# A Strassen-form input projection with attention pipelined over heads, in a two-layer hybrid decoder

## The chip, the cores and the metric

The kernel runs on one core of a Trainium2 chip. The time is the device time of one launch in microseconds (us), median of several runs; lower is better. Five engines work side by side, each in the order of its own queue: TensorE (PE, with its weight loads listed as PEld), VectorE (DVE), ScalarE (ACT), GpSimd (POOL) and SyncE (SP, which issues the DMAs).

## The reference, cut to what matters

```python
D_MODEL, SEQ, DEPTH = 2048, 512, 2            # 8 heads; q rank 512, kv rank 256, rope 64
h = layernorm(x, emb_ln_g, emb_ln_b)
for l in range(DEPTH):
    proj = h @ w_in[l]                        # 512 x 2048 @ 2048 x 4928
    (q_lat, kv_lat, k_rope, g_mla, p_in, g_pool, c_h, c_b, c_c, g_conv) = split(proj)
    y_mla  = mla_mixer(q_lat, kv_lat, k_rope, ...) * silu(g_mla)      # causal attention, 8 heads
    y_pool = pool_mixer(p_in, w_pool, pool_scale) * silu(g_pool)      # windows 2, 4, 8, 16
    y_conv = conv_mixer(c_h, c_b, c_c, conv_w) * silu(g_conv)         # b * conv3(c * h)
    out = concat(y_mla, y_pool, y_conv) @ w_out[l] + b_out[l]
    h = layernorm(ALPHA * h + out, ln_g[l], ln_b[l])
```

All numbers are float32. Of the 4928 columns of `w_in`, 4608 are 18 pairs of 128-column tiles (q 2 pairs, attention gate 4, pooling 4, convolution 8), and 320 are the kv latent and the rotary key.

## The kernel before, in words

Every large product is made from two float32r parts of each operand: `split` (L79) has ACT cast to the high part and DVE subtract it for the low part, and `mm3` (L99) issues three matmuls (lines L101, L102, L103): high times high, high times low, low times high. The 128 x 128 stationary operand is loaded anew for each.

The normalised residual lies transposed, features on partitions, in `XH` and `XL`: 16 row tiles of 128 features by 512 tokens. Weights come in blocks of 1024 columns per partition through `unit` (L83): SP loads a `raw` tile (2 buffers), ACT casts, DVE subtracts, into a ring `dunit` of 5. `in_steps` (L167) makes a pair of column tiles: four such units, 16 row tiles, two `bankA` accumulators, 96 matmuls of 512 columns:

```python
for k in range(KT):                     # 16 row tiles
    if kk == 0: wh, wl = in_unit(l, col, u)
    for e in range(2):                  # two column tiles, 512 tokens each
        mm3(accs[e], wh[:, kk, es], wl[:, kk, es], XH[:, k, :], XL[:, k, :], k == 0, k == KT - 1)
    yield
```

Layer by layer: `kv_proj` (L198) makes the kv latent with tokens on partitions; two q pairs follow. Then the heads run in a written-out order (L560 to L591): `scores` (L499, softmax per block of 128 queries: L509 to L517), `turn` (L520, the transposes L524 and the split of the probabilities), `do_k`, `do_q`, `do_rope`, `do_v` and `attend` (L537). Between these, `F(n)` (L350) lets the generators in `fill` issue steps of projections that nothing waits for: the four pairs of attention gates and the first pooling pair. After the heads come the other eleven pairs with the pooling and convolution arithmetic between them (`pooled_of` L612, L663 to L686), then the output projection, 4 token tiles by 2048 columns, with residual on POOL (`resid` L706), then layer norm. The last 256 columns go one token tile at a time, so that the next layer's transposes (`ln_to_x` L133) run beside them at the places `TURN_AT` and beside `kv_proj`.

In the embedding's layer norm the first token tile is normalised, transposed and projected while the others are still loaded (L277 to L297). Nothing but `xn_dram`, the normalised residual, goes out to DRAM between.

## Time and profile before

| what | value |
|---|---|
| runs | 1485.55, 1485.9, 1486.29 us; median 1485.9 |
| profiled execution | span 1470.5 us from first to last instruction; the launch's time of the runs is 15.4 us above this span |
| PE | 1437.9 us busy, 98%, 7202 matmuls |
| DVE | 708.3 us, 48%, 1185 instructions |
| ACT | 553.0 us, 38%, 863 |
| POOL | 215.4 us, 15%, 193 |
| DMA | 160.51 MB, 109 GB/s |

The profiled execution has no time of its own beside its span; the 15.4 us around it are taken from the median. Busy time of an engine counts overlapping instructions once. A matmul's own duration is longer than the distance to the next one, so the cost of a run of matmuls is read from their start times.

### The profile page before, as it was taken

What the parts mean: (1) busy time and instruction counts of PE and PEld (TensorE: products, weight loads), DVE (VectorE), ACT (ScalarE), POOL (GpSimd) and SP (SyncE); (2) the same over time, 40 slices, a digit from 0 to 9 for tenths busy, and PEclk for the clock granted to TensorE, in tenths of its full rate; (3) what the DMA queues carried; (4) which work ended last, traced back from release to release, by engine and by line L of the source; (5) the groups of instructions that cost most, each with busy time, mean ns of one, the idle gap of its engine ahead of it and who ended that gap; (6) DMA issues with size and microseconds to landing.
All of it is one profiled execution on the core that took longest, in us unless ns stands there. A gap on an engine that the chain in (4) does not pass through costs nothing.

```text
span 1470.5 us, 18166 instructions
## 1 busy us (share of the span) xinstructions
PE 1437.9 (98%) x7202; PEld 1225.9 (83%) x7202; DVE 708.3 (48%) x1185; ACT 553.0 (38%) x863; POOL 215.4 (15%) x193
## 2 busy tenths in 40 slices
PE   6999999999999999999999999999999999999995
PEld 6888888888888888888998888888888888888895
DVE  7745666553232253534563465666432323524338
ACT  7636466442222233212253375545232222512211
POOL 3011000012000005800001100000300000094004
PEclk9999999999999999999999999999999999999998
DMA  8522223133333345533433232132433333733333
GB/s 290 147 84 76 69 80 85 47 107 100 87 100 100 97 128 193 164 105 114 145 103 99 73 92 58 51 86 66 114 100 99 90 99 101 251 118 118 101 115 115
DMA packets 131104, 160.51 MB, mean 109 GB/s; under 512 B 13920, under 2 KB 109388, under 8 KB 127948
## 3 DMA queue, kind: packets, MB, share of 16 engines
q1 hardware_dynamic: 131020, 159.36, 35.6%
q8 instruction: 56, 0.92, 0.3%
q14 instruction: 28, 0.23, 0.1%
HBM read 146.76 MB, written 12.58 MB: 108 GB/s over the span
## 4 chain that ended last, share of the span: by engine, by line
PE 77%; issue 10%; POOL 5%; DVE 4%; ACT 3%; DMA 1%; SPq 0%; ACTq 0%; DVEq 0%; POOLq 0%
PE bankA L101 20%; PE bankA L102 20%; PE bankA L103 20%; PE bankB L103 5%; PE bankB L101 5%; PE bankB L102 5%; POOL M L711 2%; POOL M L710 2%; PE bankB L524 1%; PE bankB L142 1%; POOL scr L345 1%; DVE M L787 1%; ACT scr L514 1%; POOL scr L344 1%; DVE dunit L81 1%
## 5 line engine op out<-in xcount | busy, mean ns | idle before, releaser
L81 DVE TENSOR_TENSOR dunit<-raw,dunit 128x1024 fp32r<-128x1024 f32 (+2 forms) x229 | 291.0, 1273 | 475.6 <-ACT dunit L80 475.6
L101 PE MATMUL bankA<-XH,dunit 128*128 128x512 f32 x1152 | 451.3, 392 | 0.0
L103 PE MATMUL bankA<-XH,dunit 128*128 128x512 f32 x1152 | 449.1, 390 | 0.0
L102 PE MATMUL bankA<-XL,dunit 128*128 128x512 f32 x1152 | 449.0, 390 | 0.0
L80 ACT CAST dunit<-raw 128x1024 fp32r<-128x1024 f32 (+2 forms) x229 | 237.3, 1038 | 548.7 <-PE bankA L103 383.6
L103 PEld LDWEIGHTS bankA<-XH,dunit 128*128 128x128 f32 x1152 | 216.2, 188 | 45.2
L102 PEld LDWEIGHTS bankA<-XL,dunit 128*128 128x128 f32 x1152 | 216.4, 188 | 42.7
L101 PEld LDWEIGHTS bankA<-XH,dunit 128*128 128x128 f32 x1152 | 216.3, 188 | 42.4
L101 PE MATMUL bankA<-dunit,XH 128*128 128x512 f32 (+1 forms) x376 | 139.0, 370 | 1.0 <-ACT XH L80 1.0
L102 PE MATMUL bankA<-dunit,XH 128*128 128x512 f32 (+1 forms) x376 | 138.0, 367 | 1.0 <-POOL dunit L244 1.0
L103 PE MATMUL bankA<-dunit,XL 128*128 128x512 f32 (+1 forms) x376 | 138.0, 367 | 0.0
L710 POOL TENSOR_TENSOR M<-M,ag 128x512 f32<-128x512 f32 x32 | 48.3, 1538 | 270.6 <-ACT ag L700 270.6
L103 PE MATMUL bankB<-dunit,XL 128*128 128x512 f32 (+1 forms) x256 | 86.0, 336 | 0.0
L102 PE MATMUL bankB<-dunit,XH 128*128 128x512 f32 (+1 forms) x256 | 86.0, 336 | 0.0
L101 PE MATMUL bankB<-dunit,XH 128*128 128x512 f32 (+1 forms) x256 | 86.0, 336 | 0.0
L101 PEld LDWEIGHTS bankA<-dunit,XH 128*128 128x128 f32 x376 | 71.3, 190 | 11.7 <-ACT XH L80 1.7
L102 PEld LDWEIGHTS bankA<-dunit,XH 128*128 128x128 f32 x376 | 71.4, 190 | 11.2 <-POOL dunit L244 1.3
L103 PEld LDWEIGHTS bankA<-dunit,XL 128*128 128x128 f32 x376 | 71.2, 189 | 10.4 <-DVE XL L81 0.4
L344 POOL TENSOR_TENSOR scr<-scr,sinT 128x512 f32<-128x512 f32 x10 | 13.0, 1297 | 275.2 <-ACT scr L341 257.1
L101 PEld LDWEIGHTS bankB<-dunit,XH 128*128 128x128 f32 x256 | 48.6, 190 | 5.1
L102 PEld LDWEIGHTS bankB<-dunit,XH 128*128 128x128 f32 x256 | 48.6, 190 | 5.0
L103 PEld LDWEIGHTS bankB<-dunit,XL 128*128 128x128 f32 x256 | 48.6, 190 | 5.0
(200 smaller groups left out, 1834.7 us busy)
## 6 DMA issues: line engine op xcount, KB each, us to landing
raw<-in_w_in_dram SPq DMA_DIRECT2D x144, 512.0 KB, 3.8
raw<-in_w_out_dram SPq DMA_DIRECT2D x64, 512.0 KB, 3.8
M<-xn_dram SPq DMA_DIRECT2D x8, 1024.0 KB, 4.9
xn_dram<-M SPq DMA_DIRECT2D x6, 1024.0 KB, 4.3
raw<-in_w_ukv_dram SPq DMA_DIRECT2D x8, 512.0 KB, 3.8
raw<-in_w_uq_dram SPq DMA_DIRECT2D x32, 128.0 KB, 2.3
...
```

The source lines that it names most:

```text
L80: nc.scalar.copy(hi, src)
L81: nc.vector.tensor_sub(lo, src, hi.bitcast(F32))
L101: nc.tensor.matmul(acc, lhsT=ah, rhs=bh, start=first, stop=False)
L102: nc.tensor.matmul(acc, lhsT=ah, rhs=bl, start=False, stop=False)
L103: nc.tensor.matmul(acc, lhsT=al, rhs=bh, start=False, stop=last)
L142: nc.tensor.transpose(out=ps[:, (n * j + i) * P:(n * j + i + 1) * P], in_=rs[i][:, k // 4, (k % 4) * P:(k % 4 + 1) * P], identity=ident)
L344: nc.gpsimd.tensor_mul(sw, sw, sinT)
L345: nc.gpsimd.tensor_add(res, res, sw)
L514: nc.scalar.activation(pe[:, :W], s[:, :W], AF.Exp, bias=st[:, 1:2], scale=rs[:, qb:qb + 1], accum_out=st[:, 2:3])
L524: nc.tensor.transpose(out=pt[:, j * P:(j + 1) * P], in_=pe[:, j * P:(j + 1) * P], identity=ident)
L710: nc.gpsimd.tensor_mul(rt[t][:, cs], rt[t][:, cs], ag[:, cs])
L711: nc.gpsimd.tensor_add(rt[t][:, cs], rt[t][:, cs], ab[:, cs])
```

## The change

The tokens are halved (256 each), a pair's columns are halved (128 each), the 16 row tiles are halved into even and odd ones. Each pair is then a 2 x 2 by 2 x 2 block product, made with Strassen's seven products instead of eight. The sums of input blocks are made once per layer (`turn_steps`, `sums`: `A11`, `S5` from the first token half; `S2`, `N22`, `S1`, `S7`, `S6` once the second half is there), those of weights in every unit (`unit_of`: three POOL sums through two `sm` buffers, four splits), and `finish` puts the output blocks together from four banks, five DVE instructions and two ACT copies. For the first four pairs the products 5 and 3, which need the first token half alone, are made ahead (`pre_steps`, `prefix`) while the second half is turned; `pair_steps` then makes the other five.

All 18 pairs now come before attention, q last. Pooling and convolution results (`mix_dram`) and attention gates (`gate_dram`) go to DRAM and are loaded again. Attention has no projection between; `prep` of head h+2 and `scores` of head h+1 stand around `attend` of head h. One arena `AR` and seven blocks of 16 KB take the place of the pools. The output projection starts with the pooling and convolution rows.

```diff
-            for e in range(2):
-                es = slice(e * P, (e + 1) * P)
-                mm3(accs[e], wh[:, kk, es], wl[:, kk, es], XH[:, k, :], XL[:, k, :], k == 0, k == KT - 1)
...
+    rawp = ctx.enter_context(tc.tile_pool(name="rawp", bufs=3))
+    smp = ctx.enter_context(tc.tile_pool(name="smp", bufs=2))
+    tqp = ctx.enter_context(tc.tile_pool(name="tqp", bufs=6))
+    tdp = ctx.enter_context(tc.tile_pool(name="tdp", bufs=2))
...
+        E1, O1 = eo(1)
+        comb("S2", ALU.add, E1, O1)
...
+        comb("S1", ALU.add, E0, O1)
+        comb("S7", ALU.subtract, O0, O1, nc.vector)
+        comb("S6", ALU.subtract, E1, E0)
...
+        else:
+            t0 = tq()
+            v = t0.rearrange("p i (k q c) -> p i k q c", k=2, q=2)
+            split(v[:, 0], v[:, 1], rq[:, :, 0::3])
...
+            s = smt()
+            sv = s.rearrange("p (k n) -> p k n", k=2)
+            nc.gpsimd.tensor_sub(sv, raw.rearrange("p (k h n) -> p k h n", k=2, h=2)[:, :, 0],
+                                 raw.rearrange("p (k h n) -> p k h n", k=2, h=2)[:, :, 1])
+            t1 = tq()
+            split(t1[:, 0, :], t1[:, 1, :], s)
...
+        s = smt()
+        nc.gpsimd.tensor_add(s[:, :256].rearrange("p (k c) -> p k c", k=2), rq[:, :, 0], rq[:, :, 3])
+        t2 = tdp.tile([P, 2, 256], F32R, name="td", tag="td")
+        split(t2[:, 0, :], t2[:, 1, :], s[:, :256])
...
+        nc.gpsimd.tensor_add(s.rearrange("p (a c) -> p a c", a=4), rw[:, :, 0], rw[:, :, 1])
+        t3 = tq()
+        split(t3[:, 0, :], t3[:, 1, :], s)
...
+    def product(banks, q, w, j):
+        b, side = BANK[q]
+        bh, bl = [S[XOF[q]][:, i, j, :] for i in range(2)]
+        mm3(banks[b][:, 256 * side:256 * (side + 1)], w[0], w[1], bh, bl,
+            j == 0 and q in OPENS, j == 7 and q in CLOSES)
...
+        for u in range(4):
+            W = unit_of(l, col, u, rest)
+            for k in range(2):
+                for q in "24176" if rest else "5234176":
+                    product(banks, q, W[q][k], 2 * u + k)
+                yield
...
+        nc.scalar.copy(EG[:, 1:3], two[0])
+        nc.scalar.copy(EG[:, 0::3], two[1])
+        nc.vector.tensor_add(cv[:, 1], EG[:, 0], EG[:, 3])
+        nc.vector.tensor_add(cv[:, 2], EG[:, 1], EG[:, 2])
+        nc.vector.tensor_sub(EG[:, 0:2], EG[:, 0:2], EG[:, 2:4])
+        nc.vector.tensor_add(cv[:, 0::3], two[2], EG[:, 0:2])
+        nc.vector.tensor_add(cv[:, 0::3], cv[:, 0::3],
+                             banks[3][:, 0:256].unsqueeze(1).broadcast_to([P, 2, 256]))
...
+        for h in range(NH):
+            for qb in range(4):
+                turn(h, qb)
+            if h + 1 < NH:
+                for qb in range(4):
+                    scores(h + 1, qb)
+            attend(h)
+            if h + 2 < NH:
+                prep(h + 2)
```

How the order of instructions moves, at three places.

DVE, in the convolution pairs of the first layer. `dunit` and `raw` are the weight unit and its load, `uc` and `mscr` the convolution's tiles. Before:

```order
L81 TENSOR_TENSOR dunit<-raw,dunit 128x1024 x8
L671 TENSOR_TENSOR uc<-bankA,mscr 128x512 x2
L674 TENSOR_SCALAR mscr<-uc,vec 128x512 x2
L675 SCALAR_TENSOR_TENSOR mscr<-uc,vec,mscr 128x512 x2
L676 SCALAR_TENSOR_TENSOR mscr<-uc,vec,mscr 128x512 x2
L81 TENSOR_TENSOR dunit<-raw,dunit 128x1024 x4
```

Of the change, for the same pair (L333 to L337 are `finish`, L116 the subtraction in `split`):

```order
L116 TENSOR_TENSOR tq<-raw,tq 128x512
L334 TENSOR_TENSOR AR<-AR 128x256
L333 TENSOR_TENSOR AR<-AR 128x256
L335 TENSOR_TENSOR AR<-AR 128x512
L116 TENSOR_TENSOR tq<-sm,tq 128x512
L336 TENSOR_TENSOR AR<-bankB,AR 128x2x256
L116 TENSOR_TENSOR td<-sm,td 128x256
L337 TENSOR_TENSOR AR<-AR,bankB 128x2x256
L116 TENSOR_TENSOR tq<-sm,tq 128x512
L557 TENSOR_TENSOR AR<-AR 128x512 x2
L560 TENSOR_SCALAR AR<-AR,vec 128x512 x2
L561 SCALAR_TENSOR_TENSOR AR<-AR,vec 128x512 x2
```

One subtraction of 1024 columns per unit became four, of 512, 512, 256 and 512, three of them from a POOL sum (`sm`); `finish` is new, and the convolution reads its gate from SBUF (`AR`) where it read a bank.

POOL, from the last pooling sums to the residual in the first layer. Before:

```order
L622 TENSOR_TENSOR ps_3110<-ps_3107 128x524
L621 MEMSET ps_3113 128x8
L622 TENSOR_TENSOR ps_3113<-ps_3110 128x520
L670 MEMSET uc 128x2 x2
L710 TENSOR_TENSOR M_80<-M_80,ag 128x512
```

Of the change, two units within that stretch (L267, L274, L280 are the three sums of `unit_of`):

```order
L267 TENSOR_TENSOR sm<-raw 128x512
L274 TENSOR_TENSOR sm<-raw 128x256
L556 MEMSET AR 128x2
L494 MEMSET AR 128x1
L494 MEMSET AR 128x2
L556 MEMSET AR 128x2
L494 MEMSET AR 128x8
L280 TENSOR_TENSOR sm<-raw 128x512
```

POOL had nothing but two small fills between the pooling and the residual; now every unit of every pair has three sums there.

PE, between two blocks of scores of one head. `kh`, `qnh` and so on are keys and queries, `XH` with `dunit` is a projection. Before:

```order
L508 MATMUL bankB<-KL,SB 128x256
L101 MATMUL bankA<-XH,dunit 128x512
L102 MATMUL bankA<-XL,dunit 128x512
L103 MATMUL bankA<-XH,dunit 128x512
L101 MATMUL bankA<-XH,dunit 128x512
L102 MATMUL bankA<-XL,dunit 128x512
L103 MATMUL bankA<-XH,dunit 128x512
L101 MATMUL bankB<-kh,qnh 128x384
```

Of the change (`KQ` holds keys and queries, `RR` the rotary queries, L724 are transposes of probabilities):

```order
L706 MATMUL bankA<-KHL,RR 128x256
L707 MATMUL bankA<-KHL,RR 128x256
L120 MATMUL bankA<-KQ 128x256
L121 MATMUL bankA<-KQ 128x256
L724 MATMUL bankB<-ct,AR 128x128 x4
L122 MATMUL bankA<-KQ 128x256
L706 MATMUL bankA<-KHL,RR 128x256
L707 MATMUL bankA<-KHL,RR 128x256
L120 MATMUL bankA<-KQ 128x384
```

The projection steps that stood between two blocks of scores are gone; the only other matmuls there are the same head group's transposes.

## Rows read from the trace of the kernel before

**Rows 1.** The page: span, busy time by engine, clock, chain by engine.

```profile
span 1470.5 us, 18166 instructions
...
PE 1437.9 (98%) x7202; PEld 1225.9 (83%) x7202; DVE 708.3 (48%) x1185; ACT 553.0 (38%) x863; POOL 215.4 (15%) x193
...
PEclk9999999999999999999999999999999999999998
...
PE 77%; issue 10%; POOL 5%; DVE 4%; ACT 3%; DMA 1%; SPq 0%; ACTq 0%; DVEq 0%; POOLq 0%
```

**Rows 2.** Windows: start, the dense middle, tail; columns as the first line says.

```profile
core 0: us, PE busy (x) PEld busy (x) DVE busy (x) ACT busy (x) POOL busy (x), PEclk, DMA share, GB/s
0.00:15.00 15.00, 3.99 (x18) 3.49 (x18) 7.47 (x18) 6.62 (x10) 3.31 (x10) 1.00 0.85 284
15.00:1452.30 1437.30, 1433.93 (x7185) 1222.41 (x7185) 687.12 (x1149) 543.33 (x850) 203.90 (x178) 1.00 0.35 107
1452.30:1470.50 18.20, 0.00 (x0) 0.00 (x0) 13.70 (x19) 3.04 (x4) 8.20 (x6) 0.61 0.33 124
```

**Rows 3.** Timeline of PE, output projection: start us, duration us, instruction.

```profile
645.98 0.39 PE L101 MATMUL bankA<-dunit,XH 128*128 128x512 f32 x1
...
646.66 0.39 PE L101 MATMUL bankA<-dunit,XH 128*128 128x512 f32 x1
...
689.90 0.28 PE L101 MATMUL bankB<-dunit,XH 128*128 128x256 f32 x1
...
690.26 0.28 PE L101 MATMUL bankB<-dunit,XH 128*128 128x256 f32 x1
```

**Rows 4.** Windows: heads with their five pairs; the other eleven pairs.

```profile
100.00:306.00 206.00, 204.84 (x1055) 173.82 (x1054) 121.92 (x280) 115.94 (x212) 16.61 (x13) 1.00 0.25 70
306.00:545.00 239.00, 239.00 (x1060) 198.02 (x1059) 85.64 (x97) 61.83 (x73) 14.48 (x26) 1.00 0.36 100
```

**Rows 5.** DVE groups by line: count, then busy us, mean ns, idle before.

```profile
L81 DVE TENSOR_TENSOR dunit<-raw,dunit 128x1024 fp32r<-128x1024 f32 x216 | 279.6, 1297 | 449.4 <-ACT dunit L80 449.4
L81 DVE TENSOR_TENSOR XL<-M,XH 128x512 fp32r<-128x512 f32 x32 | 21.6, 689 | 8.9 <-ACT XH L80 8.9
...
L675 DVE SCALAR_TENSOR_TENSOR mscr<-uc,vec,mscr 128x512 f32<-128x512 f32 x8 | 5.6, 746 | 0.0
...
L674 DVE TENSOR_SCALAR mscr<-uc,vec 128x512 f32<-128x512 f32 x8 | 3.5, 479 | 0.0
L717 DVE TENSOR_TENSOR M<-bankA,M 128x256 f32<-128x256 f32 x8 | 3.3, 417 | 7.1 <-PE bankA L103 7.1
```

**Rows 6.** POOL: six sums of 512 columns in a row; two more sizes by line.

```profile
587.69 7.54 POOL L711 TENSOR_TENSOR M<-M,ab 128x512 f32<-128x512 f32 x6
...
L345 POOL TENSOR_TENSOR scr<-scr 128x512 f32<-128x512 f32 x10 | 19.8, 1977 | 2.9 <-DVE scr L343 2.1
...
L244 POOL TENSOR_TENSOR dunit<-kvraw,dunit 128x320 fp32r<-128x320 f32 x6 | 5.0, 867 | 3.4 <-ACT dunit L241 3.4
```

**Rows 7.** Timeline of POOL and DVE in the last layer norm, both at SBUF operands.

```profile
1438.63 1.55 POOL L782 TENSOR_TENSOR M<-M,dunit 128x512 f32<-128x512 f32 x1 [1.12 <-ACT M L780]
1440.26 1.62 POOL L783 TENSOR_TENSOR M<-M,dunit 128x512 f32<-128x512 f32 x1
...
1440.65 1.78 DVE L782 TENSOR_TENSOR M<-M,dunit 128x512 f32<-128x512 f32 x1
1442.46 0.69 DVE L783 TENSOR_TENSOR M<-M,dunit 128x512 f32<-128x512 f32 x1
```

**Rows 8.** The same two engines at 607 us, DVE with one operand in PSUM.

```profile
607.83 0.67 DVE L717 TENSOR_TENSOR M<-bankA,M 128x512 f32<-128x512 f32 x1
...
607.89 1.29 POOL L711 TENSOR_TENSOR M<-M,ab 128x512 f32<-128x512 f32 x1
```

**Rows 9.** Timeline of PE: a block's transposes in attention; the start.

```profile
210.86 0.63 PE L524 MATMUL bankB<-ct,scr 128*128 128x128 f32 x4 [0.24 <-DVE scr L517]
...
8.07 0.28 PE L250 MATMUL bankB<-ct,ve 32*128 32x32 f32 x1 [8.07 <-DMA ct<-in_consts_dram]
10.27 3.68 PE L142 MATMUL bankB<-ct,M 128*128 128x128 f32 x16 [1.91 <-ACT M L227]
14.97 0.64 PE L101 MATMUL bankA<-dunit,XH 128*128 128x320 f32 x1 [1.03 <-ACT XH L80]
```

**Rows 10.** DMA issues on the page: KB each, us to landing.

```profile
raw<-in_w_in_dram SPq DMA_DIRECT2D x144, 512.0 KB, 3.8
```

More of the change, by code (lines that the diff above doesn't have):

```diff
@@ L125, in ln_stats, with tok @@
         return mv[:, 0:1], rstd
[L127 to L145 removed]
+    def tok(t, c=None):
+        return ar(D * t, D) if c is None else ar(D * t + 512 * c)
@@ L156, in weave, with run @@
+    def run(*gens):
+        for g in gens:
+            for _ in g:
+                pass
     def weave(main, side, at):
@@ new lines, in prefix, with main, rope @@
+    def prefix(l, vg, vb):
+        pre = [[] for _ in range(N_PRE)]
+        def main():
+            for (_, col), banks in zip(PAIRS, pre):
+                yield from pre_steps(l, col, banks)
+        weave(main(), turn_steps(1, vg, vb), PRE_AT)
+        return pre
+    def rope(ps, res, sw):
+        for o in range(0, P, 64):
+            nc.scalar.copy(sw[o:o + 32, :], ps[o + 32:o + 64, :])
+            nc.scalar.copy(sw[o + 32:o + 64, :], ps[o:o + 32, :])
+        nc.vector.tensor_mul(res, ps, cosT)
+        nc.gpsimd.tensor_mul(sw, sw, sinT)
+        nc.gpsimd.tensor_add(res, res, sw)
+        return res
@@ new lines, in load_x, with to_vec @@
+    def load_x(t):
+        for c in range(4):
+            nc.sync.dma_start(tok(t, c), x[0, t * P:(t + 1) * P, 512 * c:512 * (c + 1)])
+    def to_vec(tl, n, at):
+        vps = bankA()
+        nc.tensor.transpose(out=vps[:, :n], in_=tl, identity=ident[:n, :n])
+        nc.vector.tensor_copy(vec[:, at:at + n], vps[:, :n])
+    ve, vr = rawt(), rawt()
+    load_x(0)
+    for row, v in ((V_EG, emb_ln_g), (V_EB, emb_ln_b)):
+        nc.sync.dma_start(ve[row:row + 16, :P], v.rearrange("(a p) -> a p", p=P))
@@ new lines, in do_q, with prep @@
+        def do_q(h):
+            qnh, qnl = KQ[:, h % 2, 2, :], KQ[:, h % 2, 3, :]
+            ps = bankB()
+            for k in range(4):
+                wh, wl = parts(wq[h // 2][k // 2], 256 * (k % 2) + P * (h % 2))
+                mm3(ps, wh, wl, QHL[:, 0, k, :], QHL[:, 1, k, :], k == 0, k == 3)
+            split(qnh, qnl, ps)
+            qn[h] = (qnh, qnl)
+        def prep(h):
+            if h % 2 == 0:
+                load_kv(h // 2)
+                load_q(h // 2)
+            do_k(h)
+            if h % 2 == 0:
+                do_rope(h // 2)
+            do_q(h)
+            if h % 2 == 0:
+                do_v(h // 2)
@@ new lines, in hybrid_trunk @@
+        prep(0)
+        acc = bankB()
+        for t in range(NT):
+            nc.tensor.matmul(acc[:, t:t + 1], lhsT=sq[0][:, t * P:(t + 1) * P], rhs=ones,
+                             start=(t == 0), stop=(t == NT - 1))
+        rs = small(NT, "rs")
+        nc.vector.tensor_scalar(rs, acc[:, 0:NT], 1.0 / QR, RMS_EPS, op0=ALU.mult, op1=ALU.add)
+        nc.gpsimd.tensor_tensor(rs, rs, half, op=ALU.pow)
+        nc.vector.tensor_scalar(rs, rs, SM_SCALE, None, op0=ALU.mult)
+        for qb in range(4):
+            scores(0, qb)
@@ new lines, in hybrid_trunk @@
+        prep(1)
+        for h in range(NH):
+            for qb in range(4):
+                turn(h, qb)
+            if h + 1 < NH:
+                for qb in range(4):
+                    scores(h + 1, qb)
+            attend(h)
+            if h + 2 < NH:
+                prep(h + 2)
+            elif h + 2 == NH:
+                XP += [block(f"XP{2 + i}", [P, 4, 2, T]) for i in range(2)]
+                for k in range(8):
+                    m = ar(3072 + 512 * (k % 2))
+                    nc.sync.dma_start(m, mix_dram[k])
+                    split(*xparts(8 + k), m)
@@ new lines, in omm, with wout @@
+        def omm(acc, t, k, w, first, last):
+            tb = slice(t * P, (t + 1) * P)
+            xh, xl = xparts(k)
+            mm3(acc, xh[:, tb], xl[:, tb], w[0], w[1], first, last)
+        def wout(k0, nk, c0, n):
+            raw = rawt()
+            nc.sync.dma_start(raw.rearrange("p (a b) -> p a b", a=nk), wo_v[:, k0:k0 + nk, c0:c0 + n])
+            return raw
+        for c in range(3):
+            accs = [bankA() if c % 2 == 0 else bankB() for _ in range(NT)]
+            for u in range(8):
+                k0 = ORDER[2 * u]
+                ts = halves(wout(k0, 2, 512 * c, 512))
+                for kk in range(2):
+                    for t in range(NT):
+                        omm(accs[t], t, k0 + kk, parts(ts[kk], 0, 512), u + kk == 0, u == 7 and kk == 1)
+            for t in range(NT):
+                evac(t, accs[t], 512 * c, 512, c)
@@ L800, in shape_consts @@
+        if not last:
+            run(side)
+            pre = prefix(l + 1, V_LG, V_LB)
 def shape_consts():
```

1116 lines of the change are left out of this document (529 added, 587 removed).

## The prediction

> **What bounds the kernel now.** Read the page first: PE is busy 98% of the span, the clock row is at full speed throughout, and 77% of the chain that ended last is PE's [rows 1]. Then the windows: between 15.0 and 1452.3 us PE is never idle for long (1433.9 of 1437.3 us), while DVE works 687 us and POOL 204 us [rows 2]. So time is lost only to columns that PE streams, 15 us ahead of them and 18 us behind, and DVE, ACT and POOL have room that costs nothing. The timeline gives PE's prices, as distances between starts: three matmuls of 512 columns take 646.66 - 645.98 = 0.68 us, 0.227 each; three of 256 columns 0.36 us, 0.120 each [rows 3]. Half the columns cost 53%, not 50%. The clock is 1.00 in both stretches, which is the 2.4 GHz level, so no row says that it will change.
>
> Whether the saving arrives is a question to DVE and POOL, which take over the block sums. Three prices matter. POOL makes a sum of 512 columns every 1.25 us when alone ((7.54 - 1.29) / 5), and 320 columns in 0.87 us [rows 6, 8]; that is 2.2 ns a column, so 256 columns are about 0.73 us, 0.69 in a row. DVE needs 0.69 us for 512 columns, 0.42 for 256, 0.75 for the three-operand form, 0.48 with one operand [rows 5]. And they don't run side by side: in the last layer norm a DVE product of two SBUF tiles takes 1.78 us beside POOL and the next instruction of that size 0.69, and POOL's starts are 1.63 us apart [rows 7]. With one operand in PSUM it takes 0.67 us while POOL works undisturbed in 1.29 [rows 8]. So an SBUF sum on DVE adds about 0.4 us to POOL's row (1.63 - 1.25), and POOL blocks DVE nearly in full. The Trainium skill's page "SBUF — State Buffer" (Who interferes with whom) has this as a lock held for the whole instruction. By that a pair of such instructions would take 1.29 + 0.69 = 1.98 us; the row's 1.63 says that their ends overlap, and I go by the row.
>
> **A, the columns.** A pair took 96 x 0.2267 = 21.76 us and takes 7 x 8 x 3 = 168 x 0.120 = 20.16. Over 36 pairs this removes **57.6 us**. The kv latent has 192 matmuls of 320 columns either way. The Trainium skill, "TensorE: Matmul & The Clock Gate" (Back-to-back issue gap), gives N / 2.4 + 2.5 ns. By that formula the pair would save 20.72 - 18.34 = 2.37 us and all of them 85; the rows' 0.227 and 0.120 decide here.
>
> **B, the 14 full pairs of a layer.** A unit is a quarter of a pair, 5.04 us on PE. It now wants three POOL sums (512, 256, 512) and four DVE splits (512, 512, 256, 512), all with SBUF operands. Without a gap POOL needs 3.19 us and DVE adds 3 x 0.4 + 0.13: 4.5 us. With nothing overlapped it is 5.8. I take 5.1, between them: only two `sm` buffers stand between POOL and the splits, so POOL's third sum waits for a cast and a split of the first. `finish` costs DVE 0.42 + 0.42 + 0.69 in SBUF and twice 0.69 from PSUM, 2.9 us a pair; what it adds to the row of the two engines is at least 0.7; I take 1.4. The convolution's DVE work (5.3 us for `cc`, 1.4 each for `cb` and `gc`, two of each a layer) now reads SBUF instead of banks, 0.9 us a pair over 14. Sum 4 x 5.1 + 1.4 + 0.9 = 22.7, against PE's 20.16: +2.5 a pair, **+71** for 28. The ends are 0 (4.5 a unit, under PE) and +200 (5.8 and the whole of `finish`). ACT's casts are cheap here. The writes to `mix_dram` and `gate_dram` stand on SP ahead of weight loads and wait for DVE; I cost them at nothing, because three `raw` buffers, some 15 us of units, cover them. Without that cover each would cost a landing, 3.8 us [rows 10].
>
> **C, the first four pairs with their head start.** In the prefix PE has 192 x 0.120 and 32 transposes of 0.12 (four in 0.63 us, of which 0.27 is the last one's own length [rows 9]): 27 us. POOL and DVE have eight units of 1.25 + 0.8 and, for the second token half, four rounds of three POOL sums, one DVE sum, four splits and two of 256 columns: 6 us a round. That makes 41 us, 54 without overlap; I take 48, because the transposes' evacuations come between on DVE: +21. The five remaining products are 120 matmuls, 3.6 us a unit, but still want sums of 256, 256 and 512 and four splits: 3.4 to 4.7 us; I take 4.0. With `finish` and the pooling arithmetic (13 us) the four pairs need 82, PE 60: +22. Per layer +43, **+86** in all; ends +38 and +136.
>
> **D, attention.** The stretch of 206 us [rows 4] holds five pairs of 21.76, so the heads' own matmuls are 97 us. PE stayed full there because a wait for the softmax was filled with those pairs. DVE was busy 121.9 us, of which 20 unit splits of 1.30 [rows 5] were the pairs': 96 are the heads'. The change adds eight splits of the outputs and eight of the reloaded branches, 11 us: 107. So DVE, not PE, is the longest engine once the pairs are gone, and the chain from scores over maximum, exponential, scaling and transposes back to PE has only `prep` and `attend` to hide under. At 107 with no gap the stage loses 10; at three quarters of that speed 48. I take 122, +25, since the neighbouring head covers much. Another 6 are lost at its entry, where the first head waits for the last q pair. **+62** for two layers; ends +24 and +108.
>
> **E, start, boundary, q.** The first projection stood at 15.0 us after one normalised tile [rows 9]. Now two tiles must be normalised and 32 transposes evacuated: about 25, +10. At the layer boundary the second half's sums wait for the last tile's norm, +4; and the q pair takes the four banks that the kv latent still occupies, +5 a layer. **+24**; ends 12 and 40.
>
> **The sum.** -57.6 + 71 + 86 + 62 + 24 = +185. Against the profiled execution, 1470.5 + 185 = 1656; what lies around a span was 15.4 us (median 1485.9), so 1671 us. All low ends give 1502, all high ones 1912.
>
> **Rivals.** *Faster.* POOL's sums and the splits stay under PE nearly everywhere: B is 0, C 10, D 20, E 10, so -18, 1468 us. For it: DVE and POOL were idle over half of the time, and a unit without gaps is 4.5 us against 5.04. Against: the prefix and the first four pairs need more than PE's time even without a gap, and attention's DVE work exceeds its PE work. It decides only if all added waits together stay below 57.6 us. *Milder.* The two engines alternate without gaps, so B is 0 and only C (50), D (40) and E (20) count: +52, 1538 us. The 1.63 us speaks for it, the two buffers against. *Worse.* Every sum shuts out the other engine for its whole length, so a unit is 1.29 + 0.73 + 1.29 + 3 x 0.69 + 0.42 = 5.8 us. Then B is 28 x (4 x 5.8 + 2.3 - 20.2) = +149; with C 110 and D 80 it is 1791 us. Against it stands the overlap in [rows 7]; for it, that gaps in a chain over three engines have the same effect. This is the lock of the Trainium skill's page on SBUF, named above, taken to the letter.
>
> **How the numbers follow.** 0.2%, some 3 us, is about what a measurement of this kernel can tell from no change. The forecast (1600 to 1760) has 0.58, the milder case 0.20, the worse one 0.12, the faster one 0.08; 0.02 is left for a time within 0.2%. The range of 8 in 10 leaves out the faster case and the worse one beyond 1770, and begins at 1510, where all the waits are near their low ends.
>
> **What would show it.** Right: POOL busy some 700 us, with mean durations of its sums well above 1.29 us; DVE's 512-column splits at a mean near 1 us in place of 0.69; PE idle inside pairs with DVE as the releaser, a full pair at 22 to 24 us in the windows; PE idle behind the scores in attention; the prefix at about 48 us. PE's starts must stay 0.120 apart within a product. Wrong: full pairs at 20.2 us with PE dense (B falls), or attention under 110 us (D falls). If POOL's sums keep to 1.29 us with DVE at 0.69, the exclusion that I read does not hold for these operands, and the kernel would be near 1470.

## The result, and the profile after

The change makes the kernel slower: median 1717.4 us (four runs, 1716.6 to 1719.8) against 1485.7 (four runs, 1473.4 to 1486.3), ratio 1.159, 95% interval 1.153 to 1.165. The forecast was 1671 us, its range 1510 to 1770. The profiled execution spans 1715.4 us, 244.9 more than before; this is the difference that the stages below have to give. The kernel before runs at two levels, near 1472 and near 1486 us, and its profiled span of 1470.5 us belongs to the lower one (beside the last experiment a run of 1472.3 us has this span and one of 1486.7 us a span of 1484.9), so about 2 us lie around a span and not 15.4.

The page of the changed kernel, against [rows 1]:

```profile
span 1715.4 us, 26050 instructions
...
PE 1492.9 (87%) x9794; PEld 1378.7 (80%) x9794; DVE 1203.6 (70%) x1971; ACT 735.4 (43%) x1473; POOL 789.7 (46%) x666
...
PEclk9788999999999999999987899999999999999998
...
PE 25%; DVE 23%; POOL 22%; issue 20%; ACT 8%; DMA 1%; POOLq 0%; SPq 0%; ACTq 0%; DVEq 0%
```

PE's share fell from 98 to 87%, and of the chain that ended last only 25% are PE's; DVE and POOL have 45% of it, where they had 9%. The clock row, full throughout before, has weak places at the beginning of each layer.

Windows by stage, against [rows 2, 4]; bounds are the first and last matmul of each stage. A full pair makes all seven products, a rest pair the five that the prefix left. In order: start; the prefix up to the second half's first product; the rest of the prefix; the four rest pairs; the twelve full pairs; the two q pairs; attention; then of the second layer the boundary with its prefix, the rest pairs, the full pairs, the q pairs and attention.

```profile
core 0: us, PE busy (x) PEld busy (x) DVE busy (x) ACT busy (x) POOL busy (x), PEclk, DMA share, GB/s
0.00:30.00 30.00, 8.68 (x35) 6.66 (x35) 20.86 (x38) 13.26 (x22) 8.14 (x13) 1.00 0.88 265
30.00:58.80 28.80, 16.83 (x107) 14.82 (x107) 22.34 (x42) 14.88 (x29) 11.05 (x13) 0.92 0.46 133
58.80:97.40 38.60, 25.07 (x116) 23.34 (x117) 30.25 (x37) 16.86 (x33) 24.85 (x24) 0.66 0.32 88
97.40:183.10 85.70, 68.72 (x489) 66.72 (x488) 56.52 (x86) 34.47 (x76) 51.34 (x53) 0.86 0.36 99
183.10:471.50 288.40, 260.56 (x2025) 250.26 (x2024) 225.58 (x306) 123.06 (x235) 181.26 (x151) 0.98 0.34 99
...
499.60:551.20 51.60, 45.18 (x350) 43.45 (x350) 35.17 (x51) 24.75 (x50) 31.43 (x28) 0.97 0.28 78
551.20:689.50 138.30, 124.75 (x670) 107.69 (x669) 111.53 (x299) 86.72 (x204) 16.06 (x11) 0.95 0.29 87
...
859.80:934.70 74.90, 49.22 (x315) 46.12 (x314) 62.92 (x91) 38.29 (x73) 44.10 (x39) 0.77 0.35 101
934.70:1019.50 84.80, 69.50 (x489) 67.03 (x488) 58.12 (x87) 34.92 (x77) 51.71 (x54) 0.86 0.37 104
1019.50:1303.40 283.90, 260.90 (x2024) 252.11 (x2023) 218.42 (x293) 122.00 (x233) 180.67 (x151) 0.97 0.35 99
...
1331.60:1383.60 52.00, 47.33 (x350) 45.69 (x350) 35.47 (x51) 24.67 (x50) 31.81 (x28) 0.90 0.29 85
1383.60:1521.30 137.70, 124.68 (x670) 107.63 (x669) 111.44 (x299) 86.62 (x204) 16.05 (x11) 0.95 0.28 82
```

The twelve full pairs took 288.4 us where twelve times 168 x 0.120 is 241.9; the prefix 67.4 (28.8 + 38.6) where 48 was forecast. The groups by line show DVE's splits and two of POOL's three sums above the prices of [rows 5, 6] and of the prediction (0.69 us; on POOL 1.29 us for 512 columns beside nothing, 0.73 for 256); the first sum, L267, keeps its own duration:

```profile
L116 DVE TENSOR_TENSOR tq<-sm,tq 128x512 fp32r<-128x512 f32 (+2 forms) x320 | 309.5, 968 | 204.3 <-ACT tq L115 203.7
...
L280 POOL TENSOR_TENSOR sm<-raw 128x512 f32<-128x512 f32 x144 | 202.7, 1407 | 158.8 <-DVE tq L116 156.9
L274 POOL TENSOR_TENSOR sm<-raw 128x256 f32<-128x256 f32 x144 | 145.8, 1012 | 89.0 <-DVE tq L116 78.4
L267 POOL TENSOR_TENSOR sm<-raw 128x512 f32<-128x512 f32 x112 | 146.0, 1304 | 22.4 <-DVE tq L116 10.4
```

Side by side in a full pair, timeline of POOL and then of DVE, against [rows 7]:

```profile
434.21 1.28 POOL L267 TENSOR_TENSOR sm<-raw 128x512 f32<-128x512 f32 x1 [0.36 <-DVE td L116]
436.12 0.74 POOL L274 TENSOR_TENSOR sm<-raw 128x256 f32<-128x256 f32 x1 [0.63 <-DVE tq L116]
...
441.38 1.12 POOL L274 TENSOR_TENSOR sm<-raw 128x256 f32<-128x256 f32 x1 [0.63 <-DVE tq L116]
```

```profile
434.65 1.38 DVE L116 TENSOR_TENSOR tq<-sm,tq 128x512 fp32r<-128x512 f32 x1
...
440.18 1.12 DVE L116 TENSOR_TENSOR tq<-sm,tq 128x512 fp32r<-128x512 f32 x1 [1.84 <-ACT tq L115]
441.22 0.68 DVE L116 TENSOR_TENSOR tq<-raw,tq 128x512 fp32r<-128x512 f32 x1
```

DVE's split of 434.65 lies beside POOL's sum, which ends at 435.49; the split ends 0.54 us after that, at 436.03: of the 0.68 us that such a split takes alone, at most 0.14 can have passed before. In turn POOL's sum of 256 columns at 441.38, issued while DVE works until 441.90, takes 1.12 us where the one at 436.12, ahead of DVE, takes 0.74, and so ends 0.60 us after DVE. The last layer norm of before shows the same in [rows 7]: POOL's product of 1440.26 ends at 1441.88, and DVE's, begun beside it, ends 0.55 us later, at 1442.43. The Trainium skill, "SBUF — State Buffer" (Who interferes with whom), describes an exclusive lock for just this pair of instructions; this trace agrees, with these numbers.

A unit of the last full pairs, from one first POOL sum to the next, without and with `finish` beside it:

```profile
444.51:449.56 5.05, 5.05 (x44) 5.05 (x44) 3.22 (x4) 2.17 (x4) 3.79 (x5) 1.00 0.38 104
449.56:456.29 6.73, 6.73 (x58) 6.65 (x57) 5.97 (x9) 3.37 (x7) 3.71 (x5) 1.00 0.29 80
```

So a plain unit takes 5.05 us, no more than PE's own 42 x 0.120 = 5.04, although ACT, DVE and POOL wait for each other and not for PE in it; one with `finish` takes 6.7. A pair with nothing else beside it takes 22.0 us, one beside the convolution's `cc` arithmetic 26.5, and the first, beside the pooling sums of the two wide windows on DVE, 30.7.

### The profile page after: what moved, and what is told of

Same layout as the page of the kernel before. It is cut to its first block, busy times and chain, and to the rows that moved or that the text cites. A ratio compares the mean times of both kernels' runs of the same rounds, so it can differ in the third digit from the quotient of the medians.

```text
span 1715.4 us, 26050 instructions
## 1 busy us (share of the span) xinstructions
PE 1492.9 (87%) x9794; PEld 1378.7 (80%) x9794; DVE 1203.6 (70%) x1971; ACT 735.4 (43%) x1473; POOL 789.7 (46%) x666
## 4 chain that ended last, share of the span: by engine, by line
PE 25%; DVE 23%; POOL 22%; issue 20%; ACT 8%; DMA 1%; POOLq 0%; SPq 0%; ACTq 0%; DVEq 0%
DVE tq L116 9%; POOL sm L280 8%; POOL sm L274 6%; ACT tq L115 4%; PE bankB L122 4%; PE bankB L121 4%; PE bankB L120 4%; PE bankA L120 4%; PE bankA L121 3%; PE bankA L122 3%; DVE td L116 2%; POOL AR L795 2%; POOL sm L213 1%; POOL AR L796 1%; DVE AR L334 1%
## 5 line engine op out<-in xcount | busy, mean ns | idle before, releaser
L116 DVE TENSOR_TENSOR tq<-sm,tq 128x512 fp32r<-128x512 f32 (+2 forms) x320 | 309.5, 968 | 204.3 <-ACT tq L115 203.7
L116 DVE TENSOR_TENSOR tq<-raw,tq 128x512 fp32r<-128x512 f32 (+2 forms) x348 | 272.8, 793 | 161.8 <-ACT tq L115 161.3
L115 ACT CAST tq<-sm 128x512 fp32r<-128x512 f32 (+2 forms) x320 | 189.2, 591 | 380.7 <-POOL sm L280 316.4
L115 ACT CAST tq<-raw 128x512 fp32r<-128x512 f32 (+2 forms) x348 | 201.2, 585 | 243.8 <-PE bankA L122 119.1
L280 POOL TENSOR_TENSOR sm<-raw 128x512 f32<-128x512 f32 x144 | 202.7, 1407 | 158.8 <-DVE tq L116 156.9
L122 PE MATMUL bankB<-S,tq 128*128 128x256 f32 x640 | 188.3, 294 | 16.9 <-DVE tq L116 16.9
L120 PE MATMUL bankB<-S,tq 128*128 128x256 f32 x640 | 187.7, 293 | 3.5 <-DVE AR L336 3.2
L274 POOL TENSOR_TENSOR sm<-raw 128x256 f32<-128x256 f32 x144 | 145.8, 1012 | 89.0 <-DVE tq L116 78.4
L121 PE MATMUL bankB<-S,tq 128*128 128x256 f32 x640 | 185.2, 289 | 0.0
L122 PE MATMUL bankA<-S,tq 128*128 128x256 f32 x512 | 155.7, 304 | 26.2 <-DVE tq L116 26.1
L120 PE MATMUL bankA<-S,tq 128*128 128x256 f32 x512 | 156.7, 306 | 22.8 <-ACT tq L115 15.7
L267 POOL TENSOR_TENSOR sm<-raw 128x512 f32<-128x512 f32 x112 | 146.0, 1304 | 22.4 <-DVE tq L116 10.4
L121 PE MATMUL bankA<-S,tq 128*128 128x256 f32 x512 | 152.4, 298 | 0.0
L122 PEld LDWEIGHTS bankB<-S,tq 128*128 128x128 f32 x640 | 126.9, 198 | 21.6 <-DVE tq L116 21.5
L120 PEld LDWEIGHTS bankB<-S,tq 128*128 128x128 f32 x640 | 126.8, 198 | 7.9 <-DVE AR L336 4.4
L122 PEld LDWEIGHTS bankA<-S,tq 128*128 128x128 f32 x512 | 105.1, 205 | 32.5 <-DVE tq L116 32.5
L120 PEld LDWEIGHTS bankA<-S,tq 128*128 128x128 f32 x512 | 106.2, 207 | 29.0 <-ACT tq L115 21.6
L121 PEld LDWEIGHTS bankB<-S,tq 128*128 128x128 f32 x640 | 126.9, 198 | 0.1
L120 PE MATMUL bankA<-tq,XP 128*128 128x512 f32 (+1 forms) x288 | 110.2, 388 | 14.1 <-ACT tq L115 11.0
L121 PE MATMUL bankA<-tq,XP 128*128 128x512 f32 (+1 forms) x288 | 110.6, 384 | 0.0
L122 PE MATMUL bankA<-tq,XP 128*128 128x512 f32 (+1 forms) x288 | 109.6, 382 | 0.0
```

The costliest lines, as they stand in the source:

```text
L115: nc.scalar.copy(hi, src)
L116: nc.vector.tensor_sub(lo, src, hi.bitcast(F32))
L120: nc.tensor.matmul(acc, lhsT=ah, rhs=bh, start=first, stop=False)
L121: nc.tensor.matmul(acc, lhsT=ah, rhs=bl, start=False, stop=False)
L122: nc.tensor.matmul(acc, lhsT=al, rhs=bh, start=False, stop=last)
L267: nc.gpsimd.tensor_sub(sv, raw.rearrange("p (k h n) -> p k h n", k=2, h=2)[:, :, 0], raw.rearrange("p (k h n) -> p k h n", k=2, h=2)[:, :, 1])
```

## Experiments

All but the last are single runs. So stages of the profiles are compared first, and a launch with 1717 on its own only where the difference is well above 14 us. Stages are those of the first layer unless said otherwise, from first to last matmul.

**Without the weight sums.**

```diff
-            nc.gpsimd.tensor_sub(sv, raw.rearrange("p (k h n) -> p k h n", k=2, h=2)[:, :, 0],
...
-            split(t1[:, 0, :], t1[:, 1, :], s)
+            split(t1[:, 0, :], t1[:, 1, :], raw[:, :512])
```

(and the same for the other two sums of a full unit)

> The full units leave out the three block sums of the weights: their splits read slices of the raw tile, so POOL has nothing to do in a full pair or a rest pair; the products keep their number and size, and the prefix keeps its own sums. Theory A (the sums, through POOL and its collision with DVE at SBUF, make a unit longer than PE's 5.04 us): the twelve full pairs behind the rest pairs fall from 288 and 284 us to 242 to 252, DVE's 512-column splits go back to a mean near 0.69 us, the launch takes 1717 - 2 x (40 + 8 + 10) = some 1600 us. Rival (the sums are hidden, and the finish, the branches on DVE or the 256-column matmuls themselves set a pair): the twelve pairs stay above 275, the launch above 1680.

1567.1 us. The windows of rest pairs and of the twelve full pairs:

```profile
97.50:158.80 61.30, 59.59 (x488) 58.86 (x488) 44.22 (x87) 34.70 (x78) 14.14 (x19) 1.00 0.51 144
158.80:402.10 243.30, 243.30 (x2025) 243.04 (x2024) 168.24 (x304) 119.29 (x232) 3.35 (x10) 1.00 0.40 116
```

PE is dense, a pair takes 20.1 to 20.2 us (the first 21.5), the clock stays at 1.00. So term A holds (the columns cost what the rows said), `finish` and the branches alone cost next to nothing, and leaving the sums out takes 150 us off the launch. That is 33 us more than expected: the twelve pairs fell to 243 us as they should, but the rest pairs gave another 24 us. What is left, a span 95 us above that of the kernel before although the columns are saved, lies in start, prefix and attention.

**Four `sm` buffers.**

```diff
-    rawp = ctx.enter_context(tc.tile_pool(name="rawp", bufs=3))
-    smp = ctx.enter_context(tc.tile_pool(name="smp", bufs=2))
+    rawp = ctx.enter_context(tc.tile_pool(name="rawp", bufs=2))
+    smp = ctx.enter_context(tc.tile_pool(name="smp", bufs=4))
```

> Four sm buffers in place of two, paid for by two raw tiles in place of three. Theory 'buffers' (POOL to ACT to DVE and back to POOL through two buffers is the chain that sets 5.5 us a unit): twelve full pairs 250 to 262 us in place of 288, POOL's waits for DVE's splits nearly gone, launch 1620 to 1670. Theory 'ports' (DVE and POOL shut each other out of SBUF, so that the sum of their work sets the unit): the waits move from POOL to the instructions' own durations, twelve pairs 275 to 290, launch within 20 us of 1717. If the two raw tiles now starve the units, waits for the load of raw show it and the launch is above 1717.

1703.6 us; the twelve pairs and POOL's groups:

```profile
175.50:457.20 281.70, 257.83 (x2024) 251.84 (x2023) 273.43 (x302) 122.05 (x232) 196.55 (x148) 0.97 0.35 101
```

```profile
L280 POOL TENSOR_TENSOR sm<-raw 128x512 f32<-128x512 f32 x144 | 222.2, 1543 | 19.3 <-DVE td L116 12.9 <-DVE tq L116 5.8 <-DMA raw<-in_w_in_dram 0.6
L267 POOL TENSOR_TENSOR sm<-raw 128x512 f32<-128x512 f32 x112 | 178.9, 1597 | 41.8 <-DMA raw<-in_w_in_dram 22.9 <-DVE tq L116 16.5 <-DVE td L116 2.3
```

POOL's wait for DVE ahead of the third sum is gone (158.8 to 19.3 us), but the sums themselves now take 1.54 and 1.60 us, and DVE is busy 273 of 282 us where it was 226 of 288. The wait moved into the instructions: theory 'ports'. The two more buffers were worth 7 us in twelve pairs, an undisturbed pair taking 21.6 in place of 22.0. (The smaller number of raw tiles shows as well: POOL's first sum waits 23 us for loads over the whole launch.)

**The sums on DVE.**

```diff
-            nc.gpsimd.tensor_sub(sv, raw.rearrange("p (k h n) -> p k h n", k=2, h=2)[:, :, 0],
+            nc.vector.tensor_sub(sv, raw.rearrange("p (k h n) -> p k h n", k=2, h=2)[:, :, 0],
...
-        nc.gpsimd.tensor_add(s[:, :256].rearrange("p (k c) -> p k c", k=2), rq[:, :, 0], rq[:, :, 3])
+        nc.vector.tensor_add(s[:, :256].rearrange("p (k c) -> p k c", k=2), rq[:, :, 0], rq[:, :, 3])
...
-        nc.gpsimd.tensor_add(s.rearrange("p (a c) -> p a c", a=4), rw[:, :, 0], rw[:, :, 1])
+        nc.vector.tensor_add(s.rearrange("p (a c) -> p a c", a=4), rw[:, :, 0], rw[:, :, 1])
```

> The three sums of a full or rest unit run on DVE in place of POOL, with the same two sm buffers. DVE's own work is then 0.69 + 0.42 + 0.69 for sums and 3 x 0.69 + 0.42 for splits, 4.3 us a unit, 17.2 a pair, 20.1 with the finish and 21.0 with the branches. Theory 'ports': without POOL each instruction keeps its own duration, the twelve pairs take 250 to 260 us, the launch 1640 to 1670, although DVE does more. Rival (POOL's help was worth having, DVE is the bound and its queue waits for ACT's casts between its own instructions): a pair takes 24 us or more, the twelve 288 or more, the launch 1717 or more.

1606.8 us, 111 less than the change; 'ports' had 1640 to 1670, so the direction is its own and the gain larger. Rest pairs and full pairs, and DVE in one of them:

```profile
96.60:166.40 69.80, 63.25 (x489) 60.96 (x488) 61.18 (x119) 34.93 (x77) 16.42 (x20) 0.98 0.43 121
166.40:420.50 254.10, 249.26 (x2024) 245.43 (x2023) 240.60 (x446) 121.86 (x234) 3.35 (x10) 0.99 0.40 113
```

```profile
386.02 0.68 DVE L116 TENSOR_TENSOR tq<-raw,tq 128x512 fp32r<-128x512 f32 x1
386.62 0.69 DVE L116 TENSOR_TENSOR tq<-sm,tq 128x512 fp32r<-128x512 f32 x1
```

DVE has 140 instructions more in the twelve pairs (446 for 306) and yet is busy only 15 us longer. Taking POOL's help away makes the stage 34 us shorter: here the two engines together are slower than one. By itself this run does not tell the exclusion from POOL's own price (1.25 us a sum, DVE 0.60), since the hand-over to POOL goes too. For the exclusion speak the durations in the changed kernel (POOL 1.12 us for 0.74 and 1.41 for 1.29, DVE 1.12 for 0.68: by estimate 0.9 us on the chain of a unit) and the run before this one. DVE's starts in a row are 0.60 us apart, not 0.69, so that its work fits under PE's and an undisturbed pair takes 20.2 us, where 21 was expected.

**No head start.**

```diff
-N_PRE = 4
+N_PRE = 0
```

> No head start: the products 5 and 3 of the first four pairs are not made ahead, the four pairs become full pairs behind the turning of the second token half. Theory (in the prefix POOL and DVE are the bound, so the head start only moves work): turning and its sums alone take 30 to 36 us, the four pairs 4 x 22.5 + 13 = 103, together 133 to 140 in place of 153 per layer, launch 1680 to 1700. Rival (the head start hides PE's work behind the turning, as its order suggests): the 4 x 48 matmuls x 0.120 = 23 us per layer come back, launch 1740 to 1765.

1701.6 us. The first four pairs end at 171.6 us instead of 183.1, and in the second layer 152.8 us behind the output projection instead of 159.7. The theory is right in sign and somewhat too large in size (11.5 and 6.9 us a layer where 13 to 20 were expected, the launch just above its 1700): products made ahead save nothing, which fits that the four pairs' splits and sums only move into a stretch that these already bound. PE's timeline behind the turning shows the clock:

```profile
75.66 0.58 PE L120 MATMUL bankA<-A,tq 128*128 128x256 f32 x1 [28.56 <-ACT tq L115]
...
82.27 0.41 PE L122 MATMUL bankA<-S,tq 128*128 128x256 f32 x1
82.48 0.41 PE L120 MATMUL bankA<-A,tq 128*128 128x256 f32 x1
...
84.17 0.28 PE L120 MATMUL bankA<-S,tq 128*128 128x256 f32 x1
84.29 0.28 PE L121 MATMUL bankA<-S,tq 128*128 128x256 f32 x1
```

After 28.6 us of idleness PE's starts are 0.21 us apart, with a granted clock of 0.50 between 76 and 83 us, the 1.2 GHz level; from 84.2 us on they are 0.12 apart with the clock at 1.00, the 2.4 GHz level.

**All sums on DVE** (on top of the sums on DVE).

```diff
-        def comb(name, op, a, b, eng=nc.gpsimd):
+        def comb(name, op, a, b, eng=nc.vector):
...
-            nc.gpsimd.tensor_sub(sv, rv[:, :, 0], rv[:, :, 1])
+            nc.vector.tensor_sub(sv, rv[:, :, 0], rv[:, :, 1])
...
-            nc.gpsimd.tensor_sub(s[:, :KVN], rv[:, 0], rv[:, 1])
+            nc.vector.tensor_sub(s[:, :KVN], rv[:, 0], rv[:, 1])
```

> Built on the kernel with the unit's sums on DVE: the sums of the prefix (those of the transposed blocks and of the products made ahead) and of the kv latent run on DVE too; POOL has no block sum left. Theory 'ports': a round of the prefix takes 9.8 us there, three POOL sums of transposed blocks and one of weights among DVE's work; with DVE alone it is 5 sums and 6 splits of 0.60 and four of 0.42 us at most, 8.2, and DVE has evacuations besides, so the prefix loses 5 to 12 us per layer, launch 1582 to 1598. Rival (in the prefix POOL's share is needed, DVE alone is longer): launch 1607 or more.

1586.6 us. The prefix ends at 88.2 instead of 96.6 us and takes 70.0 instead of 76.1 us in the second layer: as expected. That the cause is the same as in the pairs is inferred.

**Attention's low parts on POOL.**

```diff
-    def split(hi, lo, src):
+    def split(hi, lo, src, eng=nc.vector):
...
-        nc.vector.tensor_sub(lo, src, hi.bitcast(F32))
+        eng.tensor_sub(lo, src, hi.bitcast(F32))
...
-            wq[hp] = halves(raw)
+            wq[hp] = halves(raw, nc.gpsimd)
```

(and the other weight splits of attention, and `split(*xparts(8 + k), m, nc.gpsimd)`)

> The changed kernel with one edit: in attention the low parts of the weight splits and of the eight reloaded branches (33 per layer, 23 of DVE's 112 us) are made by POOL, which has little to do there. Theory D as predicted (DVE is the longest engine of the stage and the softmax waits in its queue): attention loses 6 to 15 us per layer, launch 1687 to 1705. Rival 'chain' (the latency from scores to transposes sets the waits): within 4 us of 1717. Rival 'ports' (POOL's 1.25 us instructions shut DVE's SBUF work out): attention gains 5 us or more, launch above 1725.

1714.6 us; the window of attention:

```profile
549.20:691.60 142.40, 126.02 (x666) 107.27 (x665) 102.22 (x278) 89.55 (x208) 45.59 (x36) 0.94 0.30 90
```

DVE is busy 9 us less, POOL 30 us more, and the stage is 4 us longer. So the 6 to 15 us that D's reason would have given do not come, and that reason is not borne out. It is not excluded either, since POOL's slower splits now stand in the stage: PE waits 1.8 us for one of them, and 8.3 us instead of 7.2 for DVE's splits of the values. By the launch it is 'chain', by the stage 'ports' in direction; the run does not decide between them.

**The prefix's products twice**, once with the second copy in a spare bank, once in their own accumulators.

```diff
+                spare = bankB()
+                for i, (q, t) in enumerate((("5", t5), ("3", t3))):
+                    xh, xl = [S[XOF[q]][:, p, 4 * u + jj, :] for p in range(2)]
+                    mm3(spare[:, 256 * i:256 * (i + 1)], *parts(t, P * jj), xh, xl, True, True)
```

> The changed kernel with the products 5 and 3 of the prefix made twice, the second time into a bank that nobody reads: 192 more matmuls of 256 columns per layer, 23 us of PE work at 0.120. Theory (POOL and DVE set the prefix, PE waits there): the added work hides in PE's gaps, the prefix stays within 4 us of 67.5 and 73.7, the granted clock of the prefix rises from 0.77 to 0.9 or more, launch 1710 to 1725. Rival 'clock' (the half clock in the gaps costs time on the path): with the clock held up the launch falls by 5 us or more, to 1712 or less. Rival 'PE' (PE sets the prefix): the prefix grows by 15 us or more, launch 1750 or more.

1785.7 us, the prefix ends at 129.7. As a test of PE this failed: the spare banks come from the ring that the transposes use, so each round of transposes waited for the products ahead of it. The second form has no spare bank:

```diff
-                for q, t in (("5", t5), ("3", t3)):
-                    product(banks, q, parts(t, P * jj), 4 * u + jj)
+                for rep in range(2):
+                    for q, t in (("5", t5), ("3", t3)):
...
+                        mm3(banks[b][:, 256 * side:256 * (side + 1)], *parts(t, P * jj), xh, xl,
+                            4 * u + jj + rep == 0 and q in OPENS, 4 * u + jj + rep == 8 and q in CLOSES)
```

> The changed kernel with the products 5 and 3 of the prefix made twice into their own accumulators, so that no bank is taken from the transposes; the first four pairs come out with these two products counted double. Theory (PE only waits in the prefix, and half the clock there costs nothing on the path): the 23 us of added matmuls per layer hide, the prefix stays within 5 us of 67.5 and 73.7, launch 1710 to 1730. Rival 'clock' (the half clock is on the path, and more work on PE lifts it): prefix shorter by 3 us or more, launch below 1710. Rival 'PE' (PE's part stands in series with the sums, since the transposes queue behind the products): prefix longer by 10 us or more, launch above 1740, as with the spare banks.

1764.1 us, of which 26 lie in the last output projection, behind one late load of weights, which the edit does not touch. The prefix ends at 109.7 instead of 97.4, and takes 89.0 instead of 74.9 us in the second layer: by the prefix the rival 'PE'; the launch less the 26 us is 1738, just short of its 1740. The stage shows how, first the products ahead of the transposes, then two rounds of the second half:

```profile
37.00:56.00 19.00, 19.00 (x149) 19.00 (x148) 4.88 (x11) 3.33 (x5) 2.23 (x2) 1.00 0.60 167
...
78.00:87.70 9.70, 6.26 (x48) 5.85 (x48) 5.96 (x7) 3.46 (x7) 6.36 (x7) 1.00 0.20 54
87.70:97.60 9.90, 8.97 (x48) 8.57 (x48) 7.92 (x9) 4.05 (x9) 6.45 (x7) 0.66 0.28 82
```

In the changed kernel a round is also 9.7 us, from one weight sum on POOL to the next:

```profile
66.99 1.64 POOL L306 TENSOR_TENSOR sm<-raw 128x512 f32<-128x512 f32 x1 [1.29 <-DVE S L116]
...
76.72 1.64 POOL L306 TENSOR_TENSOR sm<-raw 128x512 f32<-128x512 f32 x1 [1.14 <-DVE S L116]
```

So these rounds hide PE's double work, and the one at a granted clock of 0.66 is 0.2 us longer than the one at 1.00: there the clock costs little. What grew is mostly the part before: with twice the products the bulk of the second half's transposes begins at 56.2 us instead of 47.6, since they queue behind them, and that is 8.6 of the 12.3 us by which the prefix ends later.

**All sums on DVE, no head start.**

> All sums on DVE and no head start. Theory: turning with its sums takes 33 us with PE idle, and the first four pairs, now at nearly PE's speed, 4 x 21 + 8 = 92, together 125 per layer; with the head start (the run beside this one) prefix and rest pairs take some 60 + 68 = 128: within 10 us of that run. Rival (with DVE as the only engine of the sums, the head start has room on PE and is worth its 23 us): 15 to 45 us slower than the run beside it.

1577.5 us, 9 less than with the head start. The first four pairs end at 153.5 instead of 158.7 us. Between 54 and 64 us, where the second half's sums are made, DVE is busy 9.97 us of 10 and PE not at all: there DVE alone is now the bound.

**The next head's scores ahead of this head's transposes** (the two loops over `qb` exchanged).

> The changed kernel with the scores of the next head written ahead of the transposes of this one, so that the next softmax has these transposes and this head's value products beside it. Theory 'chain' (PE's 19 us of gaps in attention are the latency of the softmax): attention gets 3 to 10 us shorter per layer, launch 1698 to 1711. Rival (the instructions were interleaved anyway, or the keys and queries of the next head are then late instead): within 4 us of 1717, or longer.

1714.2 us; attention takes 139.9 us instead of 138.3. The rival, in the form that other data come late: PE's three waits for the values' splits (7.2 us in the changed kernel) are gone, and in their place stand waits for the splits of the probabilities (6.1 us in six) and of the rotary queries (3.5 in three).

**More evacuations on ACT** (on top of no head start).

```diff
-                if e == 0:
+                if e == 0 and j % 2 == 0:
```

> All sums on DVE, no head start, and three quarters of the evacuations of the transposes on ACT in place of half. In the stretch where the second token half's sums are made DVE is the only engine without idle time, so 4 instructions of 0.53 us less there and 4 in the first half take 2 to 5 us off per layer: launch 1568 to 1576. If ACT's casts of the sums now come late, no change from 1577.

1570.4 us, as expected: the best version found, still 6.6% above the 1472.7 us that the kernel before took beside it.

**The rotary queries last**, on top of that. The chain of waits in the changed kernel's attention gave the idea. PE's largest waits there (us in total, times, longest), DVE's timeline and PE's:

```profile
PE bankB L724 <- DVE VV L116: 7.2, 3, 2.4
```

```profile
594.15 0.69 DVE L635 TENSOR_TENSOR RR<-AR,RR 64x512 fp32r<-64x512 f32 x1 [1.23 <-ACT RR L634]
...
595.59 1.29 DVE L116 TENSOR_TENSOR VV<-bankB,VV 128x512 fp32r<-128x512 f32 x2
```

```profile
596.33 0.55 PE L724 MATMUL bankB<-ct,AR 128*128 128x128 f32 x3 [2.44 <-DVE VV L116]
...
596.97 0.41 PE L706 MATMUL bankA<-KHL,RR 128*128 128x256 f32 x1
597.18 0.41 PE L707 MATMUL bankA<-KHL,RR 128*128 128x256 f32 x1
```

The transposes wait for a bank that the values' splits release; these queue on DVE behind the rotary splits, these behind ACT and POOL. After the gap PE runs at 0.21 us for 256 columns for a while: the granted clock, 1.00 before the gap, is 0.51 from 596.9 to 597.8 us, the 1.2 GHz level, so that 2.4 us of idleness cost more than 2.4.

```diff
             do_k(h)
-            if h % 2 == 0:
-                do_rope(h // 2)
             do_q(h)
             if h % 2 == 0:
                 do_v(h // 2)
+                do_rope(h // 2)
```

> Built on the run with all sums on DVE, no head start and more evacuations on ACT (1570 us): in attention's prep the rotary queries come last, behind the values, where they stood between the keys and the other queries. Theory (the values' splits stand on DVE behind the rotary splits, these behind ACT's four copies and POOL's two products, and the transposes of the next head wait for the bank that the values' splits release, 7.2 us in three waits per layer, with half the clock behind each): the three waits go, attention gets 6 to 14 us shorter per layer, launch 1543 to 1560. Rival (the gaps only move: the scores of the next head now wait for the rotary queries, or the softmax sets the gaps): waits for RR before the scores, attention within 4 us, launch 1563 to 1578. Neither theory brings it below the kernel before.

1609.2 us (four runs, 1606.7 to 1609.9), ratio 1.091 to the kernel before (1.084 to 1.097): 39 us worse than the single run without the edit. Attention takes 146.2 us instead of 136.1, in the second layer 148.9 instead of 136.0, and PE waits elsewhere:

```profile
PE bankB L120 <- ACT PTb L115: 11.2, 3, 3.9
```

The wait for the values' splits is gone, but now ACT's casts of the next head's probabilities come late. The rival holds in kind (the gap moves) and is worse in size. Attention is 23 of the 39 us; another 11 lie in the two output projections, where PE's wait for the first weights' cast grew from 6.6 and 6.3 us to 10.4 and 10.6, and the rest in the projections; why these changed is not known. That the rotary chain blocks a queue wherever it stands is the reading that fits; that it alone sets attention's gaps was not shown.

## Why the prediction was right, and where it was not

Sign and range are right, and so is the main mechanism; the sum is 60 us short of the spans' 244.9. That the launch came out only 46 us above 1671 is luck: the 15.4 us put around the span, where about 2 belong, made up for 13 of the 60. Misses of the terms also cancel, D against B and C. Measured for both layers, from the windows above:

| term | predicted | measured | how |
|---|---|---|---|
| A columns | -57.6 | -57.6 | full pairs of 20.1 to 20.2 us once the sums are gone |
| B full pairs (q banks of E with it) | +81 | +111 | 288.4 - 241.9, 283.9 - 241.9; q pairs 51.6 and 52.0, less 40.3 each |
| C prefix and rest pairs (boundary of E with it) | +90 | +139 | 67.4 and 74.9, less 27 each; 85.7 and 84.8, less 60 each |
| D attention | +62 | +45 | 138.3 and 137.7, less 8.2 and 107 each |
| E start | +10 | +15 | first products at 30.0 instead of 15.0 |
| sum | +185 | +252 | the spans differ by 244.9; 7 us are unplaced |

**A** held, by [rows 3]. The formula that the prediction takes from the Trainium skill, "TensorE: Matmul & The Clock Gate" (Back-to-back issue gap), would have made it 85; the runs do not bear that out.

**B.** The collision read from [rows 7] is real and is most of the loss: without the sums the launch falls by 150 us, with the sums on DVE by 111. The price of a unit, 5.1 us, held where nothing stands beside it: 5.05. By that the sums would have cost nothing; what they do is to fill the chain of POOL, ACT and DVE for as long as PE works, so that whatever else DVE has to do adds to the time. Those are the terms that were too small. Units and `finish` were forecast at 21.8 us a pair and took 22.0, `finish` itself 1.9 above PE's 20.16 where 1.4 was taken. The arithmetic of the branches, taken as 0.9 us a pair, took 2.0 in the first layer and 1.6 in the second (288.4 and 283.9 less 12 x 22.05); part of it are the pooling sums on DVE, which the prediction had under C alone. Without the weight sums the same arithmetic hides under PE. That 5.1, a middle between 4.5 and 5.8, was met is partly luck: two more `sm` buffers, its reason, changed a pair by 0.4 us, and the overlap in it (1.63 us for a pair of instructions in place of 1.98) was misread from [rows 7], where 1.63 is the distance of two POOL starts and DVE's product ends 0.55 us after POOL's; in a full pair too each engine ends 0.5 to 0.6 us after the other. DVE's own price was too high by the way: 0.60 us in a row, not 0.69.

**C.** The rest pairs were right (85.7 and 84.8 for 82). The prefix was the worst step: "I take 48" against 67 and 75. It added up eight units and four rounds of 6 us as one row of work. In fact the rounds took 9.7 us each and stand in series behind 28.8 us in which tiles 2 and 3 are still normalised on DVE (work that the sum left out), and in which the transposes queue on PE behind the products made ahead.

**D.** The stage's length was right: 122 + 6 = 128 forecast; 138.3 less some 36 matmuls of the output projection that already stand in it (36 x 0.227 = 8.2) is 130.1. The term was too large, because "five pairs of 21.76" was wrong for the stretch of [rows 4]. It holds 436 matmuls of the pairs, not 480:

```profile
L101 PE MATMUL bankA<-XH,dunit 128*128 128x512 f32 x146 | 58.3, 399 | 0.0
L103 PE MATMUL bankA<-XH,dunit 128*128 128x512 f32 x145 | 56.9, 392 | 0.0
L102 PE MATMUL bankA<-XL,dunit 128*128 128x512 f32 x145 | 56.7, 391 | 0.0
```

That is 98.8 us, so the heads' own matmuls are 206 - 98.8 = 107 us, not 97. The reason, DVE as the longest engine, is not borne out: with less work on DVE the stage did not get shorter, so that its length was met is partly luck. PE's starts in the first layer's attention lie 29 us behind the prices by their sizes (138 us for 109): 18 us of this in 20 gaps, of which the three waits for DVE's splits of the values, behind the rotary chain over ACT and POOL, are the largest group (7.2 us), and 11 in smaller delays, those at the lower clock behind a gap among them. What would shorten the stage was not found.

**E**'s start took 15 us for 10. The costs taken as nothing (casts on ACT, writes to DRAM) stayed so: without the sums pairs run at PE's own time.

**The clock.** "No row says that it will change" was true of the rows and wrong for the change: the granted clock is 0.66 to 0.92 in prefix and rest pairs. In the rounds it cost some 0.2 us; what it cost elsewhere was not measured apart.
